# A Fourier and state-space encoder layer on one core: the norm weights folded into the input weights on the chip, and the split weights kept in device memory

## The chip, the core and the metric

The kernel runs on one core of a Trainium2 chip. The metric is the device time of one execution in microseconds, as the median of several runs. The engines are PE (TensorE, matrix products; PEld is its loading of the stationary operand), DVE (VectorE), ACT (ScalarE), POOL (GpSimd) and SP (SyncE, which here issues nearly all DMAs, in order). Each engine works through its own instructions in order; semaphores join them.

## What is computed

Two sequences (1024 and 2048 tokens, 1024 wide) go through one layer. Each is normalised, projected by one matrix `w_in`, and split into five parts:

```python
def rms_norm(x, w):
    y = xf * lax.rsqrt(jnp.mean(xf * xf, axis=-1, keepdims=True) + EPS)
    return (y * w).astype(x.dtype)

u = rms_norm(h, norm_w)
proj = u @ w_in
z_f, u_f, z_s, xbc, dt_raw = jnp.split(proj, [512, 1024, 2560, 5120], axis=-1)
```

`u_f` goes through a two-dimensional Fourier transform and a small mixing matrix, gated by `z_f`. `xbc` goes through a convolution of five taps and SiLU and becomes `x` (24 heads of 64), `B` and `C` (4 groups of 128); `dt_raw` (24 forward and 24 backward steps) becomes `dt` by a softplus. From these a state-space recurrence is computed forward and backward in chunks of 128 tokens, gated by `z_s` and normalised by group. Both results go through an output projection, a residual, a gated embedding and a last norm. All is in float32, to that precision.

## The kernel before

Products in float32 are made of three passes over numbers rounded for PE (float32r): a matrix `a` is split into `ah`, its rounding, and `al`, the rest, and a product is `ah bh + ah bl + al bh`. So an input weight of 1024 x 128 is split once into `wh` (a cast on ACT, L189) and `wl` (a subtraction on POOL, L190), and the normalised tokens into `uh` (ACT, L267) and `ul` (DVE, L268).

Stage 1 goes over three blocks of 1024 tokens: block 0 is the short sequence, blocks 1 and 2 the halves of the long one. Within a block the tokens lie turned (features on partitions) in three thirds of at most 342 columns, `uh0` to `uh2` and `ul0` to `ul2`, of which there is one copy each. The projection is cut into jobs of 128 output columns (`class Job`): four of `C`, four of `B`, twelve of `x`, twelve of `z`, four each of `uf` and `zf`, and one of `dt`, which is narrower and has its split weights in a tile of its own, `wdt`, loaded and split once for all blocks (L166 to L177). A job has three pieces, one for each third, of 24 matmuls (16 for `dt`) into one of three PSUM banks `ps`. That is 41 jobs or 123 pieces in a block.

The order of the work is written out by hand. One piece is a *slot*; `step` first issues what was put down for the slot with `pre`, then the piece, then what was put down with `post`. A *row* is a set of jobs whose pieces alternate, with a unit of the recurrence, the turn to the next block, or nothing attached to it. The first row of a block has `C`, `dt` and `B` (nine slots) and the chain of dt: `dt_turned` (transposes), `dt_softplus` in two parts (DVE), `dt_sums` (cumulative sums on PE, copied to `acs` by ACT, L471), `dt_rows` (transposes of `acs` on PE, `prw`, L493) and `dt_out` (stores to `ROWd` and `EXPd`). The last row of a block has `uf` 3 and `zf` 3 and brings in the next block's tokens: `x_in` loads a tile of 114 tokens, `x_norm` scales it (by the row's rstd and by the norm weight, `nwb`, in one DVE instruction, L250), `x_turn` transposes it into `uh` and `ul`.

A unit (two heads, twelve in a block) spreads over some twenty slots: rows of the decay, broadcast to all partitions, come in as `R` (L540), are cut by POOL (L548), go through an exponential on ACT (L558) and are joined on DVE (L563); POOL weights the tokens (`xw`, L587) for the states' products on PE (`pst`, L607); more rows (`er`, L635) and two outputs (L667, L669) go through SP.

Weights are loaded and split as many times as they are used, that is in every block: `weights_in` loads the raw columns into one tile `wr` (L182), `weights_split` makes `wh` and `wl`, of which there are two each. The plan (L746 to L758) splits a job's weights in the slot after the end of the job two before it, and loads the next job's raw columns one slot after a split:

```python
for m in range(2, len(coming)):
    j, k = coming[m], coming[m - 1]
    j.split_at = max(coming[m - 2].last + 1, k.split_at + 2)
    pre(k.split_at + 1, j.load)
    pre(j.split_at, j.split)
```

Tiles of the pool `t4` (six places) hold raw convolution inputs, x tiles, Fourier inputs and output weights in turn.

Stages 2 and 3 (the Fourier part; the output projection by Strassen-like sums; the embedding and the norm) are not touched.

Of the kernel before, what the change touches and what calls it, by code (L numbers as in the profile page):

```python
# [18 lines left out]
P = 128  # L19
DM = 1024  # L20
# [36 lines left out]
def tile_hybrid_encoder(ctx: ExitStack, tc: tile.TileContext, a):  # L57
# [20 lines left out]
    WSd = [dram.tile([P, 7, 4, 512], F32, name=f"WSd{i}") for i in range(3)]  # L78
    PLd = dram.tile([P, 2, DM], F32, name="PLd")
# [22 lines left out]
    with ExitStack() as ph:  # L102
        up = ph.enter_context(tc.tile_pool(name="up", bufs=1))
        wp = ph.enter_context(tc.tile_pool(name="wp", bufs=2))
        t4 = ph.enter_context(tc.tile_pool(name="t4", bufs=6))
# [19 lines left out]
        nwb = cp.tile([P, DM], F32, name="nwb")  # L125
# [35 lines left out]

        wdt = cp.tile([P, KT, 2, 64], F32R, name="wdt")

        def dt_weights_in():  # L166
            wdr = sp.tile([P, KT, 64], F32, tag="R1", bufs=3, name="wdr")
            V.memset(wdr, 0.0)
            for d in range(2):
                nc.sync.dma_start(  # L170
                    wdr[:, :, 32 * d:32 * d + 24],
                    w_in[:, C_DT + 24 * d:C_DT + 24 * (d + 1)].rearrange("(k p) c -> p k c", p=P))
            return wdr

        def dt_weights(wdr):
            S.copy(wdt[:, :, 0, :], wdr)
            V.tensor_tensor(wdt[:, :, 1, :], wdr, wdt[:, :, 0, :].bitcast(F32), op=ALU.subtract)  # L177

        def weights_in(c0):

            raw = wp.tile([P, KT, P], F32, tag="wr", bufs=1, name="wr")
            nc.sync.dma_start(raw, w_in[:, c0:c0 + P].rearrange("(k p) c -> p k c", p=P))  # L182
            return raw

        def weights_split(raw):

            wh = wp.tile([P, KT, P], F32R, tag="wh", name="wh")
            wl = wp.tile([P, KT, P], F32R, tag="wl", name="wl")
            S.copy(wh, raw)  # L189
            G.tensor_tensor(wl, raw, wh.bitcast(F32), op=ALU.subtract)  # L190
            return wh, wl
# [45 lines left out]

        def x_normed(b, i, xn):
# [11 lines left out]
            V.scalar_tensor_tensor(xt[:n, :], xt[:n, :], rs, nwb[:n, :], op0=ALU.mult, op1=ALU.mult)  # L250
# [61 lines left out]
        class Job:  # L312

            def __init__(self, B, kind, i):
                self.B, self.kind, self.i = B, kind, i
                self.c0 = {"C": C_C, "B": C_B, "x": C_X, "z": C_ZS, "uf": C_UF, "zf": C_ZF, "dt": None}[kind]
                if self.c0 is not None:
                    self.c0 += i * P
                self.dst = None
# [22 lines left out]
            def piece(self, si):  # L342
# [6 lines left out]
                if k == "dt":  # L349
                    for kt in range(KT):  # L350
                        passes = [(128, uh), (64, ul)]
                        for m, ut in passes if kt < KT - 1 else passes[::-1]:
                            T.matmul(ps[:m, :n], lhsT=wdt[:, kt, :, :].rearrange("p a c -> p (a c)")[:, :m],
# [376 lines left out]
        for bi, B in enumerate(blocks):  # L730
# [3 lines left out]
            rows_.append((B, [J("dt"), J("C"), J("B")] if bi else [J("C"), J("dt"), J("B")], "first"))  # L734
# [10 lines left out]

        n_, coming = 0, []  # L746
        for _, js, _ in rows_:
            for k, j in enumerate(js):
                j.last = n_ + 2 * len(js) + k
                if j.c0 is not None:  # L750
                    coming.append(j)
            n_ += 3 * len(js)
        coming[0].split_at = coming[1].split_at = -1
        for m in range(2, len(coming)):
            j, k = coming[m], coming[m - 1]
            j.split_at = max(coming[m - 2].last + 1, k.split_at + 2)
            pre(k.split_at + 1, j.load)
            pre(j.split_at, j.split)  # L758
# [627 lines left out]
```

## Time and profile before

| | us |
|---|---|
| median of three runs | 3041.28 |
| lowest, highest | 3039.87, 3051.15 |
| the profiled execution | 3031.59 |
| its span, first to last instruction | 3029.8 |

| engine | busy us |
|---|---|
| PE | 2836.0 |
| PEld | 2566.2 |
| DVE | 2228.9 |
| POOL | 1475.5 |
| ACT | 1389.1 |

The mean granted clock of TensorE is 0.972 of full speed. The profile is of one execution, and lines such as L361 are those of the kernel printed above. The views used below are the page (busy times, costliest groups), the busy times in stretches that one names, the list of who waited for whom (us in total, times, longest), the timeline (start, duration, engine, line, operation, result<-sources; in brackets the idle time before it and what ended it) and the list of DMA issues.

### The profile page before, as it was taken

To read this page: it belongs to the slowest core of one execution; us is meant where nothing else is said; L and a number is where in the kernel's file an instruction comes from. 1 tells how busy PE (TensorE), PEld (TensorE's weight loads), DVE (VectorE), ACT (ScalarE), POOL (GpSimd) and SP (SyncE) were. 2 spreads that over 40 slices of the span, in tenths; PEclk is the share of its full clock that TensorE was granted. 3 is DMA by queue.
4 is the path that set the end of the run, shared out by engine and by line. 5 is a ranking of instruction groups with operands and counts; after the bars stand their busy time and mean duration, and the time that the engine had idled before them with its cause. 6 is when DMAs were issued, how large, how long until landed. Compare 5 with 4: busy or idle time off the path is not lost. (4 is left out here: it accounts for less than half of the span.)

```text
span 3029.8 us, 47051 instructions
## 1 busy us (share of the span) xinstructions
PE 2836.0 (94%) x17252; PEld 2566.2 (85%) x17252; DVE 2228.9 (74%) x3412; ACT 1389.1 (46%) x2980; POOL 1475.5 (49%) x1114
## 2 busy tenths in 40 slices
PE   6899999989999899989999999969999899989998
PEld 6899989988999889989999999957677677768887
DVE  3687767666687568666779787687989988875665
ACT  4444545434544454434544444434433533354554
POOL 1355645431567565642555655455777578610000
PEclk9999999999999999999999999979999999999999
DMA  3378878972588778862677787566554644352221
GB/s 96 76 129 162 158 157 173 139 142 79 125 171 167 152 181 165 154 167 64 127 154 146 159 144 158 117 210 250 173 184 132 236 149 150 133 198 91 94 85 69
DMA packets 454579, 440.56 MB, mean 145 GB/s; under 512 B 24384, under 2 KB 405444, under 8 KB 450508
## 3 DMA queue, kind: packets, MB, share of 16 engines
q1 hardware_dynamic: 454060, 436.50, 60.6%
q8 instruction: 137, 2.24, 0.3%
q14 instruction: 94, 0.77, 0.1%
q10 hardware_dynamic: 288, 1.05, 0.1%
HBM read 328.41 MB, written 110.10 MB: 145 GB/s over the span
## 5 line engine op out<-in xcount | busy, mean ns | idle before, releaser
L361 PE MATMUL ps<-uh,wh 128*128 128x342 f32 (+1 forms) x2880 | 961.6, 334 | 8.4 <-ACT uh L267 8.4
L361 PE MATMUL ps<-ul,wh 128*128 128x342 f32 (+1 forms) x2880 | 926.3, 322 | 2.5 <-DVE ul L268 2.5
L361 PE MATMUL ps<-uh,wl 128*128 128x342 f32 (+1 forms) x2880 | 927.4, 322 | 0.4 <-POOL wl L190 0.4
L190 POOL TENSOR_TENSOR wl<-wr,wh 128x1024 fp32r<-128x1024 f32 x120 | 305.5, 2546 | 707.9 <-ACT wh L189 650.5
L361 PEld LDWEIGHTS ps<-uh,wh 128*128 128x128 f32 x2880 | 552.2, 192 | 20.1 <-ACT uh L267 9.2
L361 PEld LDWEIGHTS ps<-ul,wh 128*128 128x128 f32 x2880 | 554.5, 193 | 4.2 <-DVE ul L268 3.5
L361 PEld LDWEIGHTS ps<-uh,wl 128*128 128x128 f32 x2880 | 550.4, 191 | 1.2 <-POOL wl L190 1.1
L558 ACT ACTIVATE R<-R,lb 128x128 f32<-128x128 f32 x1152 | 356.8, 391 | 98.3 <-POOL R L548 98.2
L548 POOL TENSOR_SCALAR_AFFINE_SELECT R<-R 128x512 f32<-128x512 f32 x288 | 257.5, 905 | 193.7 <-DMA R<-ROWd 187.2
L618 DVE SCALAR_TENSOR_TENSOR H<-H,cd,pst 128x64 f32<-128x64 f32 x888 | 182.6, 274 | 47.7 <-PE pst L607 44.6
L402 DVE SCALAR_TENSOR_TENSOR xT<-raw,cvt,xT 128x1024 f32<-128x1024 f32 x144 | 214.8, 1492 | 2.6
L1102 PE MATMUL X<-whP,ah 128*128 128x512 f32 x480 | 195.2, 407 | 8.0 <-ACT pu L1111 6.4
L1102 PE MATMUL X<-wlP,ah 128*128 128x512 f32 x480 | 193.6, 403 | 1.6 <-DVE wlP L861 1.6
L1102 PE MATMUL X<-whP,al 128*128 128x512 f32 x480 | 192.5, 401 | 2.4 <-DVE al L1073 2.4
L587 POOL TENSOR_TENSOR xw<-xm,wd 128x512 f32<-128x512 f32 x144 | 181.8, 1268 | 18.7 <-PE pst L607 18.5
L367 ACT COPY raw<-ps 128x342 f32<-128x342 f32 x180 | 78.3, 438 | 241.7 <-PE ps L361 226.8
L1214 POOL TENSOR_TENSOR ht<-ht,pu 128x512 f32<-128x512 f32 x96 | 151.9, 1590 | 63.1 <-ACT pu L1111 43.0
L607 PE MATMUL pst<-xw,Bm 128*128 128x128 f32 x1056 | 151.3, 285 | 24.0 <-POOL xw L587 23.8
L607 PEld LDWEIGHTS pst<-xw,Bm 128*128 128x128 f32 x1056 | 131.9, 192 | 41.6 <-POOL xw L587 30.3
L189 ACT CAST wh<-wr 128x1024 fp32r<-128x1024 f32 x120 | 125.8, 1049 | 67.9 <-DMA wr<-in_w_in 67.2
L1073 DVE TENSOR_TENSOR al<-s,ah 128x512 fp32r<-128x512 f32 x144 | 143.6, 1021 | 16.4 <-ACT ah L1072 16.3
L563 DVE TENSOR_TENSOR R<-R,R 128x512 f32<-128x512 f32 x144 | 134.1, 931 | 25.9 <-ACT R L558 23.5
(264 smaller groups left out, 5703.9 us busy)
## 6 DMA issues: line engine op xcount, KB each, us to landing
R<-ROWd SPq DMA_DIRECT2D x288, 256.0 KB
wr<-in_w_in SPq DMA_DIRECT2D x120, 512.0 KB
er<-EXPd SPq DMA_DIRECT2D x288, 128.0 KB
Hd<-ht SPq DMA_DIRECT2D x48, 512.0 KB
ht<-Hd SPq DMA_DIRECT2D x48, 512.0 KB
y<-Yd SPq DMA_DIRECT2D x46, 512.0 KB
wlP<-WSd SPq DMA_DIRECT2D x21, 1024.0 KB
Yd<-y SPq DMA_DIRECT2D x72, 256.0 KB
```

Source lines behind the costliest of these rows:

```text
L190: G.tensor_tensor(wl, raw, wh.bitcast(F32), op=ALU.subtract)
L361: T.matmul(ps[:, :n], lhsT=wt[:, kt, :], rhs=ut[:, kt, :n], start=(i == 0), stop=(i == 3 * KT - 1))
L402: V.scalar_tensor_tensor(dst, raw[:, k:k + TB], cvt[:, 20 * k + ct:20 * k + ct + 1], dst, op0=ALU.mult, op1=ALU.add)
L548: G.affine_select(out=R.rearrange("p c h l -> p (c h) l"), in_=R.rearrange("p c h l -> p (c h) l"), pattern=[[0, 4], [sgn, P]], compare_op ...
L558: S.activation(R[:, c, h, :], R[:, c, h, :], AF.Exp, bias=self.B.lb[:, 2 * p + c, hc + h:hc + h + 1])
L563: V.tensor_tensor(E[0], E[0], E[1], op=ALU.add)
L587: G.tensor_tensor(xw, self.xm[c4].rearrange("p c (h e) -> p c h e", h=2), col(self.B.wd[:, c4:c4 + 4, hc:hc + 2]).broadcast_to([P, 4, 2, 6 ...
L607: T.matmul(pst[:, c, :], lhsT=B.Bm[self.g][:, c4 + c, :], rhs=xw[:, c, :, :].rearrange("p h e -> p (h e)"), start=True, stop=True)
L618: V.scalar_tensor_tensor(dst[:, e], H[d][:, cc, e], B.cd[:, cc, hc + h:hc + h + 1], pst[:, c, e], op0=ALU.mult, op1=ALU.add)
L1073: V.tensor_tensor(al, src, ah.bitcast(F32), op=ALU.subtract)
L1102: T.matmul(ps, lhsT=at[:, k, :], rhs=wt[:, k, :], start=(first and i == 0), stop=(i == 11), skip_group_check=not first)
L1214: return lambda t: G.tensor_tensor(h, h, t, op=ALU.add)
```

## The change

The norm weight is no longer multiplied into the tokens but into the rows of the input weights: it is loaded as eight rows of 128, turned on PE into `nwt`, a column for each of the eight k-tiles, and in block 0 each raw weight tile is scaled by eight ACT multiplies before its split. The tokens are scaled by their rstd alone, on ACT. In block 0 the split weights are stored to device memory (`WPd`, two slots after the split); in blocks 1 and 2 they are loaded from there, 2 x 512 KB in lines of 4 KB per partition, and cast in place on ACT, without POOL. There are three places for `wh` and for `wl`; in block 0 the raw tile takes one of the places of `wh`, so `wr` is gone, as are `nwb` and `wdt`; `t4` gets a seventh place. The weights of `dt` are a job's like the others. `B` has a row of its own behind the first row; in the last row the pieces are in another order; the slots of the dt chain, of the convolution of `C` 0 and of the x tiles are set anew.

```diff
+    WPd = {i: [dram.tile([P, KT, P], F32, name=f"WPd{i}_{x}") for x in range(2)] for i in range(C_DT // P)}
+    WPd["dt"] = [dram.tile([P, KT, P], F32, name="WPddt")]
...
-        wp = ph.enter_context(tc.tile_pool(name="wp", bufs=2))
-        t4 = ph.enter_context(tc.tile_pool(name="t4", bufs=6))
+        wp = ph.enter_context(tc.tile_pool(name="wp", bufs=3))
+        t4 = ph.enter_context(tc.tile_pool(name="t4", bufs=7))
...
-            V.scalar_tensor_tensor(xt[:n, :], xt[:n, :], rs, nwb[:n, :], op0=ALU.mult, op1=ALU.mult)
+            S.mul(xt[:n, :], xt[:n, :], rs)
...
+            def places(self):
+                return [wp.tile([P, KT, P], F32R, tag=f"w{x}", name=f"w{x}") for x in ("h" if self.dt else "hl")]
+
             def load(self):
-                self.raw = weights_in(self.c0)
+                if self.B.bi:
+                    self.w = self.places()
+                    for wt, kept in zip(self.w, self.kept):
+                        nc.sync.dma_start(flat(wt).bitcast(F32), flat(kept))
+                elif self.dt:
...
+                else:
+                    self.raw = wp.tile([P, KT, P], F32, tag="wh", name="wr")
+                    nc.sync.dma_start(self.raw, w_in[:, self.c0:self.c0 + P].rearrange("(k p) c -> p k c", p=P))
 
             def split(self):
-                self.w = weights_split(self.raw)
+                if self.B.bi:
+                    for wt in self.w:
+                        S.copy(flat(wt), flat(wt).bitcast(F32))
+                    return
+                raw = self.raw
+                for k in range(KT):
+                    S.mul(raw[:, k], raw[:, k], nwt[:, k:k + 1])
+                self.w = self.places()
...
+                S.copy(wh, raw)
+                (V if self.dt else G).tensor_tensor(wl, raw, wh.bitcast(F32), op=ALU.subtract)
+                for wt, kept in zip(self.w, self.kept):
+                    pre(slot[0] + 2, nc.sync.dma_start, flat(kept), flat(wt).bitcast(F32))
...
-                    conv(16 + i, self.dst, CT, s_ + (2 if i else 4))
+                    conv(16 + i, self.dst, CT, s_ + (2 if i else 3))
...
-            rows_.append((B, [J("dt"), J("C"), J("B")] if bi else [J("C"), J("dt"), J("B")], "first"))
+            rows_.append((B, [J("dt"), J("C")] if bi else [J("C"), J("dt")], "first"))
+            rows_.append((B, [J("B")], None))
...
+            if what == "last":
+                turn = [(0, 0), (0, 1), (1, 0), (0, 2), (1, 1), (1, 2)]
+            else:
+                turn = [(k, si) for si in range(3) for k in range(len(js))]
...
+            j = coming[m]
+            if j.B.bi:
+                pre(coming[m - 3].last + 1, j.load)
+                pre(max(j.first - 2, coming[m - 3].last + 2), j.split)
+            else:
+                j.split_at = max(coming[m - 2].last + 1, coming[m - 1].split_at + 2)
+                if m > 2:
+                    pre(coming[m - 1].split_at + 1, j.load)
+                pre(j.split_at, j.split)
...
-                    post(q + 7, dt_turned, B)
-                    pre(q + 8, dt_softplus, B, 0)
-                    pre(q + 9, dt_softplus, B, 1)
-                    post(s0 + 13, dt_sums, B)
-                    post(s0 + 14, dt_rows, B)
-                    pre(s0 + 16, dt_out, B)
+                    post(q + 5, dt_turned, B)
+                    pre(q + 6, dt_softplus, B, 0)
+                    pre(q + 7, dt_softplus, B, 1)
+                    post(q + 10, dt_sums, B)
+                    post(q + 12, dt_rows, B)
+                    pre(q + 14, dt_out, B)
...
-                    for i, s_ in enumerate((2, 3, 4, 4, 5, 6, 8, 9, 10)):
-                        pre(s0 + (0, 0, 1, 2, 2, 3, 5, 6, 7)[i], x_in, b, i)
+                    for i, s_ in enumerate((3, 4, 5, 5, 6, 7, 7, 8, 9)):
+                        pre(s0 + (0, 0, 1, 2, 3, 4, 5, 6, 7)[i], x_in, b, i)
```

More of the change, by code (lines that the diff above doesn't have):

```diff
@@ L123, in load_x @@
             return xt, n
-        nwb = cp.tile([P, DM], F32, name="nwb")
+        nwr = sp.tile([KT, P], F32, tag="y0", name="nwr")
+        nwt = cp.tile([P, KT], F32, name="nwt")
         tri = cp.tile([P, 2, P], F32, name="tri")
@@ L160, in tile_hybrid_encoder @@
         w_in = a["w_in"][0]
[L164 to L191, printed above, removed]
         def weight_sums(i, s0):
@@ L790, in tile_hybrid_encoder @@
             coming[0].split()
-            coming[1].load()
+            coming[2].load()
             x_in(b0, 5)
@@ L798, in tile_hybrid_encoder @@
             post(2, small_constants)
[L799 removed]
+            for i, (n_in, n_norm, n_turn) in enumerate(
+                    ((0, 0, 0), (0, 0, 0), (0, 0, 1), (0, 1, 2), (1, 2, 2), (1, 2, 3)), 3):
+                if i > 5:
+                    pre(n_in, x_in, b0, i)
                 if i > 3:
[L801 to L806 removed]
+                    pre(n_norm, x_norm, b0, i)
+                post(n_turn, x_turn, b0, i)
+            pre(8, decay_rates)
+            for (B, js, what), row in zip(rows_, pieces):
                 bi, s0 = B.bi, slot[0]
@@ L830, in tile_hybrid_encoder @@
                             pre(s0 + 2 * i, norm_piece, BLOCKS[bi + 1], i)
-                for si in range(3):
-                    for j in js:
-                        step(lambda: j.piece(si))
+                for j, si in row:
+                    step(lambda: j.piece(si))
             while before or behind_:
```

53 lines of the change are left out of this document (31 added, 22 removed).

## The prediction

> **What bounds the kernel now.** I read the page's busy times first, then the stretches of the program one by one, then PE's waits in each stretch, then the queues that feed them. The page names the engine:
>
> ```profile
> PE 2836.0 (94%) x17252; PEld 2566.2 (85%) x17252; DVE 2228.9 (74%) x3412; ACT 1389.1 (46%) x2980; POOL 1475.5 (49%) x1114
> ```
>
> PE is busy 94% of the span, and the change removes no matmul. So what it can win is PE's idle time, and the half-speed time that follows idling. The stretches (the first is the start up to the first `uf` job, then block 0, the turn to block 1, block 1, the turn to block 2, block 2, the two later stages, and a part of the last stage for a price) show where that is:
>
> ```profile
> 0.00:73.20 73.20, 48.07 (x273) 44.78 (x274) 25.67 (x51) 31.47 (x62) 7.84 (x9) 0.93 0.35 99
> 73.20:631.50 558.30, 538.09 (x3739) 518.16 (x3738) 404.97 (x681) 277.14 (x623) 281.56 (x220) 0.98 0.76 141
> 631.50:720.30 88.80, 79.22 (x537) 75.57 (x536) 51.84 (x90) 32.11 (x75) 26.78 (x20) 0.92 0.56 125
> 720.30:1300.50 580.20, 546.05 (x3761) 524.05 (x3759) 419.40 (x696) 276.52 (x619) 337.83 (x261) 0.98 0.74 153
> 1300.50:1389.10 88.60, 79.64 (x539) 75.78 (x539) 52.11 (x92) 32.25 (x75) 38.66 (x28) 0.92 0.51 137
> 1389.10:1937.60 548.50, 539.02 (x3781) 520.03 (x3780) 424.88 (x701) 256.33 (x584) 281.09 (x221) 0.99 0.69 139
> 1992.80:3029.80 1037.00, 969.84 (x4368) 773.79 (x4368) 818.64 (x1041) 468.08 (x904) 483.42 (x340) 0.97 0.45 153
> 2720.00:3020.00 300.00, 300.00 (x1397) 243.96 (x1396) 186.82 (x299) 156.08 (x302) 0.00 (x0) 1.00 0.24 83
> ```
>
> Columns: length; busy time of PE, PEld, DVE, ACT, POOL; granted clock; DMA share; GB/s. The same 108 slots (36 jobs of three pieces) take 558.3 us in block 0, 580.2 in block 1 and 548.5 in block 2, where PE idles 9.5 us. Block 1 idles 34 us, block 0 20 us. PE's waits in block 0, in the turn after it, in block 1 and in block 2 (total, times, longest):
>
> ```profile
> PE prw L493 <- ACT acs L471: 7.6, 1, 7.6
> PE pd L575 <- ACT wh L189: 3.9, 1, 3.9
> ...
> PE pst L607 <- POOL xw L587: 1.8, 3, 0.6
> ```
> ```profile
> PE pt L264 <- DVE H L618: 5.0, 2, 3.5
> PE pt L264 <- DVE xt L250: 4.4, 1, 4.4
> ```
> ```profile
> PE pst L607 <- POOL xw L587: 17.4, 11, 3.8
> PE pd L575 <- ACT wh L189: 6.2, 1, 6.2
> PE prw L493 <- ACT acs L471: 4.8, 1, 4.8
> ```
> ```profile
> PE prw L493 <- ACT acs L471: 4.8, 1, 4.8
> PE pst L607 <- POOL xw L587: 4.5, 4, 1.8
> ```
>
> Three things stand out: one wait for the cumulative sums of dt in each block (`acs`, L471), POOL's weighted tokens in block 1 (`xw`, L587), and a weight cast that ACT reached late (`wh`, L189). Each long wait costs more than itself, since the clock is halved around it; stretches at the first `acs` wait, at the second and at the `wh` wait of block 1:
>
> ```profile
> 103.30:110.10 6.80, 3.74 (x16) 3.48 (x17) 4.01 (x7) 4.88 (x8) 0.00 (x0) 0.50 0.00 0
> 748.40:755.20 6.80, 5.44 (x22) 5.17 (x23) 4.12 (x6) 6.01 (x10) 0.00 (x0) 0.50 0.00 1
> 1055.60:1062.40 6.80, 4.22 (x21) 3.92 (x22) 6.09 (x5) 2.00 (x5) 4.01 (x2) 0.50 0.82 130
> ```
>
> At clock 0.50, half of PE's busy time there is lost: 1.9, 2.7 and 2.1 us.
>
> **The dt chain.** Moving dt into a row with C alone, and B to its own row, keeps the number of slots but ends dt two slots sooner; the sums then come two slots ahead of the rows instead of one, and the softplus no longer runs against the taps of C and B at once on DVE. Two slots are about 10 us (580.2/108 = 5.4 us each), more than the longest wait, 7.6 us. In the three blocks this removes 7.6 + 4.8 + 4.8 = 17.2 us and 1.9 + 2.7 + 2.7 (the third taken as the second) = 7.3 us of clock: 24.5. I take -23, since ACT may still come late by a little; the other end is -12, if half of the waits only shrink. What is late next in these slots is DVE, whose softplus work is unchanged. The Trainium skill (TensorE: Matmul & The Clock Gate, Part 1) says that an idle window of about 3.4 us halves the clock and that a busy one of about 3.4 us restores it. By that alone each of the three waits would cost 1.7 us of clock, and this term would be 22.3 at most; the stretches above are 6.8 us wide, so the measurement decides.
>
> **The weights in blocks 1 and 2.** Each of the 40 split jobs of a block loses its subtraction on POOL and gains a second cast on ACT:
>
> ```profile
> L190 POOL TENSOR_TENSOR wl<-wr,wh 128x1024 fp32r<-128x1024 f32 x120 | 305.5, 2546 | 707.9 <-ACT wh L189 650.5 <-PE pst L607 36.6 <-PE po L649 9.2
> ```
> ```profile
> L558 ACT ACTIVATE R<-R,lb 128x128 f32<-128x128 f32 x1152 | 356.8, 391 | 98.3 <-POOL R L548 98.2
> L189 ACT CAST wh<-wr 128x1024 fp32r<-128x1024 f32 x120 | 125.8, 1049 | 67.9 <-DMA wr<-in_w_in 67.2
> ```
>
> POOL: 36 x 2.55 = 92 of 337.8 us go in block 1. More telling is the 650.5 us in which POOL, which works in order, stood before its subtraction until ACT had cast; `xw` and the row cuts are queued behind it. Without a subtraction nothing of POOL waits for a weight, and loads come four slots ahead instead of two, so the 67.2 us in which ACT stood before a cast for the DMA mostly go too. ACT gains 36 x 1.05 = 38 us on 276.5 of 580.2, which leaves it 46% idle. PE's 17.4 + 6.2 us in block 1 with 2.1 us of clock, 25.7 us, can go at most; I take -15, because R rows that land late delay POOL as well:
>
> ```profile
> POOL wl L190 <- ACT wh L189: 650.5, 102, 38.2
> POOL R L548 <- DMA R<-ROWd: 187.2, 106, 5.0
> ```
>
> Ends: -26 and +5 (the longer loads below delay R). Block 2 has 4.5 us of such waits: -2 (-4 to +6). The Trainium skill (SBUF — State Buffer, Who interferes with whom) says that a DVE instruction with two SBUF inputs and a POOL one that reads SBUF exclude each other for the whole instruction. By it the taps on DVE would win too, and block 1's term would go to its end, -26, and the sum to -35; no row here tells how much of DVE's time that is.
>
> **Block 0.** Here each job gains eight ACT multiplies of 128x128. The nearest row is L558, 356.8/1152 = 0.31 us each: 2.5 us per job, 89 us on ACT's 277 of 558. The cast, and POOL's subtraction behind it, end 2.5 us later, so `xw` behind those comes 2.5 us later; today that wait costs PE 1.8 us here, so a slack of a slot mostly covers it. SP's next raw load waits for the subtraction as it does now
>
> ```profile
> SPq L182 <- POOL wl L190: 409.3, 93, 34.1
> ```
>
> and the row, decay and output DMAs behind it on SP go 2.5 us later. Each job also stores 2 x 0.5 MB through SP, two slots after its split, when the subtraction on which the store waits is done; behind the store on SP are R's rows, on which POOL, then ACT's exponentials, DVE's join and PE's `pd` depend. The price of such a store is bounded by two rows: at the last stretch's 83/0.24 = 346 GB/s, 1.05 MB takes 3.0 us of all sixteen DMA engines; at block 0's 141/0.76 = 186 GB/s, 5.6 us. Over 36 jobs that is 109 or 203 us, against 24% of 558.3 = 134 us of unused DMA time. I take the lower price, since the stores are long contiguous lines as in the last stage: share 0.96. The queue then still keeps up, but R lands later. Estimate +12: a third of a microsecond per job, between 0 and +60. In blocks 1 and 2 a job loads 1.05 MB where it loaded
>
> ```profile
> wr<-in_w_in SPq DMA_DIRECT2D x120, 512.0 KB
> ```
>
> so 0.52 MB more, 1.6 us per job or 56 us per block of the 26% unused: covered.
>
> **The start.** The row's norm weight leaves DVE, and its scaling goes to ACT; the norm weight's broadcast load goes:
>
> ```profile
> 42.35 1.06 ACT L244 ACTIVATE junk<-xt 114x1024 bf16<-114x1024 f32 x1 [6.32 <-DMA xt<-in_x_prompt]
> ```
> ```profile
> 10.41 1.29 DVE L250 SCALAR_TENSOR_TENSOR xt<-xt,ss,nwb 114x1024 f32<-114x1024 f32 x1
> ```
> ```profile
> 21.29 0.65 PE L361 MATMUL ps<-uh,wh 128*128 128x342 f32 x1 [1.76 <-ACT uh L267]
> ...
> 29.72 0.40 PE L353 MATMUL ps<-uh,wdt 128*128 128x342 f32 x1
> ...
> 32.16 0.32 PE L353 MATMUL ps<-uh,wdt 128*128 128x342 f32 x1
> ...
> 44.65 0.65 PE L361 MATMUL ps<-uh,wh 128*128 128x342 f32 x1 [6.40 <-ACT uh L267]
> ```
>
> Ahead of the first piece ACT gets four multiplies (priced at L244's 1.06) and 2.5 us for C's weights, 6.7 us, less 2 us for the missing 0.5 MB load (1.5 to 2.8 us at the two rates above): +5. The 6.4 us wait at 44.65, due to an x tile that landed late, goes: the seventh t4 place and B's raw load, no longer held until C's split, bring x sooner; but ACT is then the bound and leaves 3 us of waits. Last, B is split only when C has ended: 2.5 + 1.05 + 2.55 = 6.1 us on ACT and POOL, covered by one dt piece of 2.8 us (29.72 to 32.48), so 3.3 us stick out. Sum +5 - 6.4 + 3 + 3.3 = +5; I take +4 (-5 to +12).
>
> **The turns.** The scaling of x moves to ACT there too, x gets later slots and PE has two pieces instead of three to cover each third. The waits on L250 and L618 go or change their name, new ones of 1 us or so arise ahead of each dt piece: 0, between -8 and +8 each. From 1992.8 on no line changes: 0.
>
> Sum: -23 - 15 - 2 + 12 + 4 = -24 us. The profiled execution took 3031.6 us, 9.7 under the median of 3041.28; -24 from the median is 3017.
>
> **Rivals.** *Block 0 becomes bound by DMA* (slower). Place: the stores among the R rows, in the queue that POOL already waits 187.2 us for. At 5.6 us per job the need is 203 - 134 = 69 us over what is free, in place of +12: the sum is +33, 3074. For it: R, broadcast rows, sets block 0's low rate. Against: the stores are not such rows. It decides from 4.7 us per job: 36 jobs then need 170 us, 36 more than are free, as much as the other terms bring. *ACT takes POOL's place* (no change): its work rises by 89 us in block 0 and 38 in each other block, PE's waits change their name to ACT, and block 1 keeps its 580: -24 + 15 + 2, -7, 3034. Against: ACT's idle half; for: `wh` waits exist. *The three places do not work as meant* (slower): if places go round in turn, a raw load of block 0 takes the place of the job two before, and SP stands until that job's last matmul, about two slots, with R queued behind it. Subtraction and `xw` then come a slot late; at 2 us per job for 36 jobs the sum is -24 + 72 = +48, 3089.
>
> **How the numbers follow.** A measurement can tell about 0.5% (15 us) from no change. Forecast 0.55, ACT 0.22, DMA 0.15, places 0.08. Of the forecast's 0.55 some 0.07 falls within 15 us; of ACT's 0.22, 0.06 is faster and 0.02 slower. So faster 0.54, same 0.22 (0.07 + 0.14 + 0.01), slower 0.24. The low end takes the gains whole (-24.5 - 26 - 4 - 5 = -59.5): 2982; the high end reaches into the DMA case: 3072. The forecast's own range, one term at a time at its far end, is 3001 (the turns) to 3037 (block 1).
>
> **What would show it.** Right: no wait on `acs`; block 1 within 570; POOL's busy time in block 1 near 246 us; POOL's wait for R in block 0 up by less than half; the first `uf` piece at 73 to 81 us. Wrong: DMA share of block 0 at 0.95 or more with PE idle over 40 us there; SP standing ten microseconds before each raw load; or waits on L189's successor on ACT as long as `xw` had.

## Result and profile after

The changed kernel took 3129.8 us (median of 4 runs, 3125.83 to 3149.84) against 3040.57 for the kernel before on the same chip: ratio 1.0301, 95% interval 1.0249 to 1.0352. It is 3% slower; the forecast was 3017, and its range ended at 3072. The profiled execution is the slowest of the four, 3149.84 us with a span of 3148.0, so its stretches add up to 118 us over before, not to the 89 between the medians.

First the engines' busy times on the page of the kernel after (its counterpart of before heads the prediction):

```profile
PE 2868.9 (91%) x17253; PEld 2599.0 (83%) x17253; DVE 2094.6 (67%) x3386; ACT 1590.6 (51%) x3417; POOL 1226.2 (39%) x1034
```

POOL lost 249 us of work, as it was meant to. DVE lost 134, of which the scaling of x (L250) is 37; nearly all the rest is the same instructions taking less time (last section). PE's share of the span fell from 94% to 91%. Then the stretches of the kernel after, with the columns of the prediction (start, block 0, turn, block 1, turn, block 2):

```profile
0.00:79.98 79.98, 49.79 (x275) 45.90 (x276) 16.29 (x48) 54.00 (x108) 7.80 (x9) 0.91 0.36 111
79.98:695.60 615.62, 555.26 (x3739) 532.04 (x3737) 401.59 (x677) 360.66 (x908) 278.58 (x220) 0.96 0.80 191
695.60:796.57 100.97, 79.64 (x537) 74.63 (x536) 46.62 (x90) 47.85 (x95) 17.91 (x17) 0.88 0.59 160
796.57:1384.03 587.46, 549.46 (x3761) 530.33 (x3759) 368.81 (x687) 307.57 (x652) 225.54 (x224) 0.97 0.75 181
1384.03:1485.62 101.59, 80.92 (x540) 75.56 (x539) 47.06 (x92) 47.28 (x90) 24.26 (x24) 0.88 0.60 156
1485.62:2045.57 559.95, 544.94 (x3783) 527.05 (x3781) 364.86 (x692) 290.22 (x621) 170.94 (x184) 0.98 0.70 169
```

Against before, the start is 7 us longer, block 0 57, the turns 12 and 13, block 1 7 and block 2 11. The remaining 10 us lie behind these stretches, nearly all in stages that no edit touches. That rest took 1089 to 1103 us in the sixteen profiles of this study, here 1102 against 1092, so its 10 us are scatter and not an effect of the change. Block 0 has the most: PE idles 60 us there (20 before), and its busy time is 17 us longer, since the granted clock stood at 0.50 for 51 us of the block (17 before). DMA is busy 80% of it. The waits of PE, POOL, ACT and SP in block 0 of the kernel after (total, times, longest):

```profile
PE pst L618 <- POOL xw L598: 41.9, 16, 5.5
```
```profile
POOL wl L334 <- ACT wh L333: 255.9, 34, 20.6
POOL R L559 <- DMA R<-ROWd: 57.0, 27, 6.0
```
```profile
ACT wr L327 <- DMA wr<-in_w_in: 69.8, 22, 7.9
```
```profile
SPq L318 <- POOL wl L334: 114.1, 29, 18.7
```

Read from below upwards, they close into a ring: SP waits for POOL's subtraction before it may load the next raw weights, ACT waits for the raw weights, POOL waits for ACT, and PE waits for `xw`, which is queued on POOL behind the subtraction. One round of it in the timeline of the kernel after (start, duration; in brackets the idle time before and what ended it), first POOL, then ACT, then SP:

```profile
309.27 2.40 POOL L334 TENSOR_TENSOR wl<-wr,wh 128x1024 fp32r<-128x1024 f32 x1 [3.54 <-ACT wh L333]
...
326.79 2.40 POOL L334 TENSOR_TENSOR wl<-wr,wh 128x1024 fp32r<-128x1024 f32 x1 [10.53 <-ACT wh L333]
```
```profile
323.18 2.45 ACT L327 ACTIVATE wr<-wr,nwt 128x128 f32<-128x128 f32 x8 [3.37 <-DMA wr<-in_w_in]
325.66 1.05 ACT L333 CAST wh<-wr 128x1024 fp32r<-128x1024 f32 x1
```
```profile
311.80 0.61 SPq L318 DMA_DIRECT2D wr<-in_w_in  x1
312.47 6.63 SPq L646 DMA_DIRECT2D er<-EXPd  x4
319.21 1.96 SPq L551 DMA_DIRECT2D R<-ROWd  x2
321.21 1.35 SPq L263 DMA_DIRECT2D WPd<-wh  x1
323.11 1.95 SPq L263 DMA_DIRECT2D WPd<-wl  x1
325.17 1.49 SPq L551 DMA_DIRECT2D R<-ROWd  x2
329.21 0.37 SPq L318 DMA_DIRECT2D wr<-in_w_in  x1
```

The subtraction ends at 311.67, the raw load goes out 0.13 us later, lands at 323.18 (11.4 us), multiplies and cast end at 326.71, the subtraction at 329.19, and the next load goes out at 329.21: 17.4 us for a round. Over the 35 raw loads of block 0 (issue and landing events of the trace) the mean round is 9.6 us of landing, 4.8 to the end of the cast, 2.5 to the end of the subtraction: 17.0, and 36 rounds are the 615.6 us of the block (17.1 each). In the kernel before the same means are 9.6, 3.2 and 2.6, 15.5 in all, and there the 3.2 hold spare time, since the cast takes 1.05. In the kernel after, multiplies and cast take 3.5 of the 4.8; in the rest the weights have landed and ACT has not come to them yet.

Block 1 looks different. There is no subtraction in it, and yet it got longer. Its waits on PE and on POOL:

```profile
PE pst L618 <- POOL xw L598: 11.8, 6, 2.8
PE pd L586 <- DVE R L575: 9.6, 2, 5.2
```
```profile
POOL R L559 <- DMA R<-ROWd: 309.5, 57, 44.9
```

`xw` fell from 17.4 us to 11.8, and the waits for `wh` and `acs` are gone, but PE now waits 9.6 us for what comes from R. POOL's 309.5 us are mostly spare time and no measure of that: POOL stood 51.2 us for R in the same block before and 174.5 for the cast, which is gone, and in the run e15 below it still stands 239.5 us for R where PE idles 10.

### The profile page after: what moved, and what is told of

The parts are those of the page before. It is cut to its first block, busy times and chain, and to the rows that moved or that the text cites. A ratio compares the mean times of both kernels' runs of the same rounds, so it can differ in the third digit from the quotient of the medians.

```text
span 3148.0 us, 47800 instructions
## 1 busy us (share of the span) xinstructions
PE 2868.9 (91%) x17253; PEld 2599.0 (83%) x17253; DVE 2094.6 (67%) x3386; ACT 1590.6 (51%) x3417; POOL 1226.2 (39%) x1034
## 3 DMA queue, kind: packets, MB, share of 16 engines
q10 hardware_dynamic: 288, 1.05, 0.1%
## 5 line engine op out<-in xcount | busy, mean ns | idle before, releaser
L559 POOL TENSOR_SCALAR_AFFINE_SELECT R<-R 128x512 f32<-128x512 f32 x288 | 232.1, 812 | 857.5 <-DMA R<-ROWd 732.2
L334 POOL TENSOR_TENSOR wl<-wr,wh 128x1024 fp32r<-128x1024 f32 x40 | 98.5, 2464 | 351.8 <-ACT wh L333 337.1
L618 PE MATMUL pst<-xw,Bm 128*128 128x128 f32 x1056 | 160.9, 297 | 66.3 <-POOL xw L598 66.0
L618 PEld LDWEIGHTS pst<-xw,Bm 128*128 128x128 f32 x1056 | 141.1, 204 | 83.8 <-POOL xw L598 74.9
L598 POOL TENSOR_TENSOR xw<-xm,wd 128x512 f32<-128x512 f32 x144 | 175.2, 1222 | 46.0 <-PE pst L618 36.6
L413 DVE SCALAR_TENSOR_TENSOR xT<-raw,cvt,xT 128x1024 f32<-128x1024 f32 x144 | 189.8, 1318 | 2.6
L663 DVE TENSOR_TENSOR yt<-po,er 128x512 f32<-128x512 f32 (+1 forms) x144 | 91.2, 634 | 87.8 <-PE po L660 66.0
```

What stands on the lines that cost most here:

```text
L334: (V if self.dt else G).tensor_tensor(wl, raw, wh.bitcast(F32), op=ALU.subtract)
L413: V.scalar_tensor_tensor(dst, raw[:, k:k + TB], cvt[:, 20 * k + ct:20 * k + ct + 1], dst, op0=ALU.mult, op1=ALU.add)
L559: G.affine_select(out=R.rearrange("p c h l -> p (c h) l"), in_=R.rearrange("p c h l -> p (c h) l"), pattern=[[0, 4], [sgn, P]], compare_op ...
L598: G.tensor_tensor(xw, self.xm[c4].rearrange("p c (h e) -> p c h e", h=2), col(self.B.wd[:, c4:c4 + 4, hc:hc + 2]).broadcast_to([P, 4, 2, 6 ...
L618: T.matmul(pst[:, c, :], lhsT=B.Bm[self.g][:, c4 + c, :], rhs=xw[:, c, :, :].rearrange("p h e -> p (h e)"), start=True, stop=True)
```

## Experiments

All edits are on the kernel after unless said otherwise. Where a stretch has the same instructions, its length repeats within 8 us: block 0 took 608.6 to 616.7 us in the six profiles that leave it untouched, block 1 584.0 to 588.7 in seven, block 2 554.3 to 560.0 in seven. Ratios are to the kernel before, timed beside each run. The fences of this section show stretches of the named kernel, columns as above. Some expectations count from other pieces: their turn of 126 us ends two jobs later than the 101 us of the fences, and their blocks 1 and 2 (562 and 559 us) begin there.

**Without the multiplies (e1).** The two lines `for k in range(KT): S.mul(raw[:, k], ...)` are out.

> The changed kernel without the eight multiplies per job that fold the norm weight in (so the norm weight is left out of the result); stores, places and all else stay. Read in block 0, from the first piece of uf to the turn, which took 558 us before and 616 us after. Theory A (ACT reaches the casts late, POOL stands before its subtraction and the weighted tokens stand behind it): block 0 comes back by 30 us or more, POOL's 256 us before wl fall under 150, PE's 42 us before xw under 15; total about 3090. Theory B (the stores fill the queue and make the raw weights and R late): block 0 comes back by less than 15 us, total 3115 or more. Theory C (the places: a raw load waits for the subtraction one job earlier, whatever ACT does): also less than 15 us.

3115.64 us, ratio 1.0265 (1.0234 to 1.0297).

```profile
72.75:671.02 598.27, 549.20 (x3738) 527.49 (x3737) 406.57 (x677) 273.78 (x616) 273.39 (x220) 0.97 0.83 194
```

Block 0 came back by 17 us, between what the theories asked, and the start by 7. POOL still stood 202.6 us before `wl`, PE 30.0 before `xw`, and ACT's wait for the raw weights rose from 69.8 to 101.1: with ACT quicker, the landing takes 10.9 us on the mean (9.3 in e3 below, which is without the stores too). The round is then 10.9 + 1.7 + 2.6 = 15.2 us, where a job takes 16.6: a raw load leaves SP 1.4 us after its place is free, so here the ring alone does not hold the block.

**Without the copies in device memory (e2).** No stores but dt's; blocks 1 and 2 load, scale and split like block 0.

> The changed kernel without the device-memory copies: no stores for any job but dt, and blocks 1 and 2 load, scale and split the raw weights as block 0 does. Theory A: block 0 stays near 600 us (under 15 back), and blocks 1 and 2 get slow like it, PE waiting 30 us or more in each for xw; total 3160 or more. Theory B: block 0 comes back to 575 or less, and blocks 1 and 2 are near 580 and 550; total 3080 to 3100. Theory C: block 0 hardly changes, blocks 1 and 2 get its lateness.

3113.89 us, ratio 1.0248 (1.0225 to 1.0271).

```profile
81.02:650.78 569.76, 540.74 (x3739) 518.06 (x3737) 398.35 (x677) 360.89 (x906) 286.67 (x220) 0.99 0.69 139
...
745.93:1350.42 604.49, 557.25 (x3761) 536.37 (x3759) 421.43 (x691) 361.76 (x908) 343.90 (x260) 0.95 0.73 146
...
1445.66:2014.38 568.72, 545.26 (x3782) 524.47 (x3781) 418.25 (x696) 343.40 (x875) 281.01 (x220) 0.98 0.71 134
```

The stores are worth 46 us of block 0 (615.6 to 569.8), more than theory A had left for them. The mean round is 7.9 + 5.3 + 2.6 = 15.8 us here, as long as a job: without the stores a raw weight lands in 7.9 us, with them in 9.6. The total falls by 16 us only, since blocks 1 and 2 now bear the multiplies.

**Neither (e3).** Both edits together.

> Neither the multiplies (norm weight left out) nor the device-memory copies: raw weights loaded, cast and split in every block as before the change, in the changed places and with the changed order of dt, the turns and x's scaling on ACT. If A and B together are the whole loss of block 0, block 0 is back at 550 to 565 us and what is left over against before are the turns (25 us) less the dt chain (20 us): 3035 to 3055. If the places are at fault (C), block 0 stays over 575 and blocks 1 and 2 go over 590 and 560: 3080 or more.

3042.09 us, ratio 1.0010 (0.9993 to 1.0027): no difference from before.

```profile
73.06:626.51 553.45, 536.58 (x3738) 517.48 (x3737) 406.77 (x677) 272.40 (x617) 282.00 (x220) 0.99 0.75 143
...
725.39:1299.14 573.75, 546.40 (x3761) 525.49 (x3759) 415.63 (x690) 274.11 (x617) 336.51 (x260) 0.98 0.74 153
...
1394.38:1938.18 543.80, 538.36 (x3782) 519.26 (x3781) 418.95 (x695) 255.99 (x585) 277.29 (x221) 1.00 0.70 139
```

The four runs make a square for block 0: 553.5 with neither, 569.8 with the multiplies, 598.3 with the stores, 615.6 with both. Multiplies cost 16 to 17 us and stores 45 to 46, each alike with and without the other (15 and 43 if the kernel after is taken at 613.0, the mean of the six profiles above); the places by themselves cost nothing (theory C, as far as it blames them alone, falls). In blocks 1 and 2 the multiplies would cost 31 and 25 us (e2 less e3), and what stands in their place, two loads and two casts for one load, a cast and a subtraction, costs 14 and 16 (after less e3).

**Raw weights by turns (e5).** This opens the ring in block 0: a raw load waits for the subtraction two jobs back.

```
-self.raw = wp.tile([P, KT, P], F32, tag="wh", name="wr")
+self.raw = wp.tile([P, KT, P], F32, tag="w" + "hl"[self.m % 2], name="wr")
...
-pre(coming[m - 1].split_at + 1, j.load)
+pre(max(coming[m - 1].split_at - 1, 0), j.load)
```

> The changed kernel with one edit for block 0: the raw weights take a third place of wh and a third place of wl by turns, and are loaded two slots earlier, so that a load waits for the subtraction two jobs back and not for that of the job before. Theory C (SP's 114 us before the raw loads and ACT's 70 us before the raw weights are the cause): both waits fall under 30 us, block 0 comes back by 25 us or more, total 3095 or less. Theory A (ACT's eight multiplies): the waits fall, but block 0 comes back by less than 15 us. Theory B (stores): the waits for the raw weights stay, moved to the queue.

3119.91 us, ratio 1.0261 (1.0228 to 1.0294). Block 0 and POOL's waits in it:

```profile
80.85:672.30 591.45, 549.04 (x3738) 527.32 (x3737) 393.00 (x677) 359.93 (x908) 270.73 (x220) 0.96 0.81 197
```
```profile
POOL wl L334 <- ACT wh L333: 168.4, 24, 24.5
POOL R L559 <- DMA R<-ROWd: 95.8, 39, 6.1
```

Block 0 came back by 24 us (21.5 from the mean of 613.0), just short of what theory C asked, and the total by 10 only, 25 short. SP's wait before the raw loads fell from 114 to 22 us, and ACT's for them is gone. The rest turned into a wait for R, where 57 us became 95.8, and into 31 us that POOL stood before the subtraction for stores to land. So the ring is one way in which the stores cost time, and R and the wait for the stores themselves are others.

**Stores on ACT's queue (e7), and the same with the ring open (e9).** `nc.sync.dma_start` becomes `nc.scalar.dma_start` for the stores, one slot later.

> The changed kernel with the stores of wh and wl issued from ACT, a slot later, and not from SP. The bytes and the sixteen DMA engines are the same; what differs is that the stores stand no more in SP's order and queue ahead of the R rows, the decays and the raw weights, at the price of ACT's time to issue them. Theory Q (the 45 us that the stores cost block 0 come from their place in SP's order and queue): block 0 comes back by 25 us or more, to 590 or less. Rival (the engines' bytes in a burst): by less than 10. Third (ACT's issue time and waits): block 0 gets longer, over 620.

> The run with raw weights by turns (block 0 there 591 us), with the stores issued from ACT a slot later. The ring of the raw weights is open in both, so what is left of the stores' cost must show in R. Theory (bytes): block 0 stays within 6 us of 591. Rival (SP's order: 1.1 us of SP's time for each store, ahead of R's loads): R's loads, 6.9 us after their slot there, come within 4.5 us and block 0 falls to 580 or less. Third (ACT's time to issue them): block 0 over 598.

e7: 3139.17 us, ratio 1.0320 (1.0297 to 1.0342), block 0 609.8: within the scatter, so theory Q falls while the ring is closed. A raw weight still lands in 9.5 us there, whichever engine issues the stores. e9: 3134.10 us, ratio 1.0308 (1.0278 to 1.0338); block 0, the wait of DVE that grew

```profile
81.89:701.16 619.27, 556.70 (x3738) 532.10 (x3737) 395.82 (x672) 359.61 (x911) 285.75 (x220) 0.95 0.76 189
```
```profile
DVE zT L248 <- ACT zT L247: 116.3, 12, 18.5
```

and, of ACT and of POOL,

```profile
ACT xT L417 <- DMA er<-EXPd: 70.9, 8, 12.9
```
```profile
POOL wl L334 <- DMA WPd<-wl: 116.0, 8, 18.4
```

R's loads did go out 2.4 us after their slot instead of 6.9, as the rival wanted, and the third theory held as well: ACT came late to its other work, DVE waited 116 us for `zT`, the gate's tile that ACT begins (35.5 in e5), and PE 52.5 us for the states `H` behind it on DVE. What ACT stood for is in the trace. The DMAs of this program, from SP and from ACT alike, use eight semaphores in turn, and an issue waits until the DMA that last used its semaphore has landed. ACT, done with its own work, stood 99 us before 19 of its stores, and each of these waits ended within 0.15 us of the landing of such an earlier load from SP (`er` for 90 of the 99 us). POOL, for its part, stood 116 us before the subtraction for stores of `wl` to land (31 us for stores in e5). The Trainium skill (DMA: Bandwidth & Descriptors, Queues, rings and completion order) says that each DMA engine takes turns between the queues that have work, packet by packet. No run here shows that by itself: R went out earlier because SP no longer issued the stores.

**No casts in blocks 1 and 2 (e8).** The matmuls read the kept weights as they land.

> The changed kernel without the two casts per job on ACT in blocks 1 and 2: the matmuls read the kept weights as they land (they were rounded when they were split). Block 0 is untouched. Blocks 1 and 2 (pieces 138 to 240 and 261 to 368) took 562 and 559 us, against 549 and 543 before. Theory (two casts, 2.1 us per job on ACT ahead of the exponentials): both come back by 8 us or more. Rival (the half megabyte more per job, and SP standing before the loads until a job's last matmul, make R late): both stay within 4 us.

3133.77 us, ratio 1.0297 (1.0274 to 1.0321). Block 1 580.5 and block 2 555.2, 7 and 5 us less, between what the theory and the rival asked, and in block 2 within the scatter: the casts are a small part at most.

**Kept loads from ACT (e10).** `nc.scalar.dma_start` for the loads of wh and wl in blocks 1 and 2.

> The changed kernel with the kept weights of blocks 1 and 2 loaded from ACT and not from SP; bytes, slots and casts as they are. In the changed kernel R's loads of block 1 were issued 8.2 us after their slot began on the mean, against 4.9 us in the kernel before with only the new dt order, and the block took 562 against 548 us. Theory (SP's order: the loads, standing until a job's last matmul, hold R's loads behind them): R's loads are issued within 6 us of their slot, blocks 1 and 2 come back by 6 us or more each, to 556 and 552. Rival (the bytes, whichever queue carries them): both within 3 us of 562 and 559. Third (ACT stands instead of SP and its exponentials come late): both longer by 5 us or more.

3163.04 us, ratio 1.0399 (1.0375 to 1.0423). Block 1, and PE's wait in it:

```profile
799.49:1404.98 605.49, 549.90 (x3760) 529.88 (x3759) 363.09 (x681) 302.22 (x653) 241.96 (x225) 0.95 0.74 177
```
```profile
PE po L660 <- DVE H L629: 54.6, 10, 11.7
```

R went out 2.6 us after its slot in block 1, from 8.2, and the block still got 18 us longer (block 2 six). The theory that SP's order alone is the cause falls; again ACT stood, 163 us before 32 of its loads, for earlier loads from SP to land, and `H` came late.

**One load per job (e15).** Blocks 1 and 2 load only wh.

```
-self.w = self.places()
-for wt, kept in zip(self.w, self.kept):
-    nc.sync.dma_start(flat(wt).bitcast(F32), flat(kept))
+self.w = [wp.tile([P, KT, P], F32R, tag="wh", name="wh")]
+nc.sync.dma_start(flat(self.w[0]).bitcast(F32), flat(self.kept[0]))
+if not self.dt:
+    self.w = self.w * 2
```

> The changed kernel, but in blocks 1 and 2 only wh is loaded for each job, 0.5 MB, and stands in for wl too (so wl's part is left out of those blocks); the cast runs twice on it, so that ACT's work is as before, and SP has one load per job to issue instead of two at the same slot. Theory (the bytes of the second load delay what is queued with them): blocks 1 and 2, 562 and 559 us in the changed kernel, come back by 12 us or more each, to 550 and 547 or less. Rival (the casts, and SP standing before a load until a job's last matmul): both within 5 us of 562 and 559.

3061.27 us, ratio 1.0052 (1.0035 to 1.0069).

```profile
789.71:1336.83 547.12, 536.66 (x3761) 518.21 (x3759) 368.18 (x687) 310.87 (x652) 228.89 (x224) 0.99 0.73 160
...
1430.45:1965.22 534.77, 534.77 (x3782) 517.67 (x3781) 364.87 (x692) 291.82 (x621) 167.22 (x184) 1.00 0.68 142
```

40 and 25 us less, with the casts as they were: the second half megabyte of each job is what blocks 1 and 2 pay for. In block 2 PE is busy without a gap. R's loads of block 1 went out 3.6 us after their slot. SP stood no less for a job's last matmul before these loads, 87 us in block 1 against 74 in the kernel after, so that part of the rival falls. The run takes out one DMA as well as its bytes, and these two are not told apart.

**The dt order alone (e4)**, on the kernel before: `[J("C"), J("dt")]` and `[J("B")]` as rows, the sums at q + 10 and the rows at q + 12, the x tiles of a turn at slots `(2, 3, 4, 4, 5, 6, 7, 8, 9)`.

> The kernel before with the new order of the dt chain alone: dt in a row with C, B in its own, the sums two slots ahead of the rows, and the x tiles turned at the slots that this order needs. Weights, scaling of x and the order of the last row are as before. Theory (the waits for the cumulative sums and the half clock after them are a real loss that the order takes away): no wait for acs in any block and 15 to 24 us less, 3015 to 3025. Rival (the dt pieces come sooner after the turn of x, and PE now waits there for uh instead): the acs waits go, waits on uh or xt of the same size come in the first six slots after the last row, total 3032 to 3042.

3027.48 us, ratio 0.9952 (0.9934 to 0.9970). From the start to block 2:

```profile
0.00:78.13 78.13, 48.40 (x275) 44.98 (x275) 30.45 (x57) 35.38 (x67) 7.82 (x9) 0.91 0.33 93
78.13:630.99 552.86, 536.38 (x3738) 516.96 (x3737) 405.17 (x676) 272.45 (x617) 280.93 (x220) 0.99 0.77 143
630.99:718.45 87.46, 78.19 (x537) 74.32 (x536) 58.93 (x96) 33.15 (x76) 26.60 (x20) 0.94 0.53 132
718.45:1291.67 573.22, 547.92 (x3761) 526.63 (x3759) 408.16 (x690) 274.46 (x617) 329.79 (x260) 0.98 0.76 154
...
1380.62:1919.71 539.09, 536.00 (x3783) 517.87 (x3781) 414.49 (x695) 254.92 (x583) 276.17 (x220) 1.00 0.68 141
```

The median is 14 us lower, just short of the theory's 15 to 24. The waits for `acs` are gone; blocks 0, 1 and 2 gain 5, 7 and 9 us, the turns do not lengthen, and the start, where x and dt now meet sooner, loses 5.

**x scaled on DVE (e6)** and **the turn's order (e11)**. e6 puts `V.tensor_scalar` in place of `S.mul` for x; e11 keeps ACT's scaling but runs the last row's pieces by turns as before and turns x at the slots of e4.

> The changed kernel with one edit: x is scaled on DVE again (by the row's norm alone) and not on ACT. It acts at the start and in the two turns only. Theory (ACT's scaling makes uh late there): the start, 80 us, falls under 77, each turn (from the last row's first piece to the end of dt and C, 126 us) falls by 4 us or more, total 8 to 15 us less. Rival (the new order and slots of the turn are the loss, whoever scales): both stay within 2 us, total unchanged.

> The changed kernel with the last row's pieces by turns as before the change, and the x tiles of the next block loaded, scaled (still on ACT) and turned at the slots of the kernel with the dt order alone, one slot sooner for the first five. Theory (the changed order frees the first third of x only after three pieces and turns it a slot later, so PE waits for uh ahead of dt and C): each turn, 126 us in the changed kernel, comes to 117 or less, total 15 to 25 us less than the changed kernel. Rival (ACT's scaling of x makes uh late at any slots): the turns stay over 122.

e6: 3129.66 us, ratio 1.0284 (1.0259 to 1.0310); the start is 76.3 us, the turns 100.3 and 95.1. e11: 3128.73, ratio 1.0278 (1.0246 to 1.0309), and its turns are

```profile
697.88:790.04 92.16, 79.48 (x537) 74.86 (x536) 47.48 (x90) 47.83 (x95) 18.44 (x17) 0.94 0.64 178
...
1378.73:1468.33 89.60, 79.53 (x539) 75.48 (x538) 47.27 (x93) 47.52 (x91) 24.14 (x24) 0.92 0.69 176
```

against 101.0 and 101.6: the order of pieces and slots gave 9 and 12 us back. Four other runs with the turns untouched by their edit (e1, e5, e7, e9) took 100.6 to 102.7 and 95.9 to 100.6, so of the second turn 6 to 12 us are the order's, and e6's 95.1 there is hardly outside the scatter. Scaling on DVE gave 4 us back at the start; an effect on the turns is not shown. The 21 us of e11's turns do not show in its median, which lies within the intervals of both; that its total is lower than the changed kernel's is not shown.

**Half of the store (e12).** The ring open in every block; kept is the scaled raw weight alone, 0.5 MB per job, and blocks 1 and 2 load it, cast it and subtract.

> As the run with raw weights by turns (block 0 there 591 us, blocks 1 and 2 560 and 554), but kept in device memory is only the scaled raw weight, 0.5 MB per job in place of 1 MB, stored as soon as it is scaled; blocks 1 and 2 load it, 0.5 MB in whole lines, and cast and split it as before the change, without multiplies. Theory (bytes: the megabyte stored per job delays raw weights and R): block 0 comes to 570 to 580, blocks 1 and 2, with the bytes of before, to 552 or less and 548 or less; total about 3060 to 3080. Rival (any store in SP's order costs the same, however long): block 0 stays over 585, blocks 1 and 2 come back all the same.

3013.32 us, ratio 0.9913 (0.9885 to 0.9941): faster than before, and 47 us lower than its theory allowed, which had left out what the open ring brings in blocks 1 and 2.

```profile
78.18:642.52 564.34, 541.60 (x3738) 519.81 (x3737) 393.64 (x677) 360.62 (x908) 281.28 (x220) 0.98 0.78 173
...
735.11:1287.80 552.69, 539.83 (x3760) 518.67 (x3759) 415.28 (x690) 273.08 (x617) 344.68 (x260) 0.99 0.78 158
...
1382.92:1918.27 535.35, 535.34 (x3782) 517.91 (x3781) 405.80 (x695) 254.69 (x585) 272.02 (x220) 1.00 0.69 141
```

Block 0 lost 27 of e5's 591 us with half of the store, and POOL's subtraction in blocks 1 and 2 does no harm: they are 35 and 25 us shorter than in the changed kernel, which was made to be rid of it.

**A version that beats both (e14).** The dt order with its turn, dt in a place, the ring open in every block, the norm weight on x, nothing kept but dt's weights.

> A version that could beat both: the new dt order with its turn, dt's weights in a place like the others, and the raw weights by turns in the third places, loaded two slots earlier in all blocks; the norm weight stays on x, on DVE, and no weights are kept but dt's. Theory (the ring raw load, landing, cast, subtraction, next raw load took 15.5 us per job before, as long as PE's three pieces; opened, it no longer holds PE): at least 8 us under the run with the dt order alone, 3008 to 3019. Rival (the ring only follows PE there, nothing is won, or R's rows are delayed by the earlier loads): 3022 to 3035.

2995.94 us, ratio 0.9854 (0.9831 to 0.9878), 31.5 us under e4's median and 12 under what its theory allowed.

```profile
73.98:621.02 547.04, 535.81 (x3738) 516.03 (x3737) 408.18 (x677) 272.03 (x617) 284.26 (x220) 0.99 0.75 144
...
711.62:1268.28 556.66, 541.16 (x3761) 520.44 (x3759) 417.30 (x690) 272.93 (x617) 339.13 (x260) 0.99 0.77 157
```

Against e4, from which it differs by the ring, the third places that open it, and dt's place, block 1 lost 17 us and block 0 six; PE's wait for `xw` in block 1 fell from 16.2 to 4.2 us. So the ring had held PE in the kernel before too, above all in block 1, as far as one run that changes the three together can tell.

## Why the prediction was wrong

**The bound** was read rightly: PE's work stayed (its instructions are the same), and all that was lost is PE idling and the slower clock around it.

**The dt chain**, -23: right in mechanism, too large. Alone it is worth 14 us (e4), and its start costs 5, which the prediction had not seen.

**Block 0**, +12: the step that failed most. "The queue then still keeps up, but R lands later. Estimate +12: a third of a microsecond per job" let the unused share of DMA time cover the stores. The price of the bytes was not at fault: DMA share times length rose by 2.3 us per job from e3 to e1 and by 2.8 from e2 to the kernel after, where the prediction took 3.0, and 17 to 20% of the DMA time stayed unused. Measured are 45 us for the stores, 1.25 us per job, and 16 for the multiplies, which "a slack of a slot mostly covers". There was no such slack: the prediction quoted SP's 409 us before the raw load and POOL's 650 before `wl` as two waits, and did not see that they follow on each other. Landing 9.6, cast 1.05 and subtraction 2.6 make 13.3 us of a 15.5 us round; 2.2 were free, the multiplies alone take 2.45, and the longer landing that the stores bring (7.9 to 9.6 us) comes on top.

**Blocks 1 and 2**, -15 and -2: of the wrong sign. "So 0.52 MB more, 1.6 us per job or 56 us per block of the 26% unused: covered" is the step that failed. The same half megabyte costs 40 and 25 us (e15), with 26% of DMA time unused before. That POOL's subtraction delays `xw` was true, but it was the ring that made it late: with the ring open, block 1 keeps the subtraction and takes 556.7 us (e14, in which dt has its place too).

**The start**, +4: +7, inside its bounds; the start is 73 us without the multiplies (e1, e3). **The turns**, 0 with at most 8 each: +12 and +13. "PE has two pieces instead of three to cover each third" was seen and priced at a microsecond; the order of pieces and slots is worth 9 us in the first and 6 to 12 in the second (e11).

**The rivals.** *Block 0 bound by DMA* was nearest in its sign and place, but not as told: it needed a DMA share of 0.95, and the share is 0.80. *ACT takes POOL's place* shows in the ring, not in blocks 1 and 2 (casts: 7 and 5 us). *The places do not work as meant*: in block 0 SP does not stand two slots for a job's last matmul (10.5 us in all for PE); the raw load leaves 0.13 us after the subtraction. The places did tie each load to the subtraction of the job before, as the single raw tile had done. The range missed because each cost was bounded alone, by busy shares, and none by the length of a round. It was also too narrow by the prediction's own terms: its end of 3072 lies below the prices of two rivals (3074 and 3089), and the forecast's own range to 3037 left out block 0's far end, which makes it 3065.

**The signs.** Three of the signs for being right came true although the forecast was 113 us off: no wait on `acs`, POOL's wait for R in block 0 up by less than half (48.1 to 57.0 us), the first `uf` piece at 80 us. Of the signs for being wrong, DMA's share stayed at 0.80, and SP stood 3.9 us before a raw load on the mean. None of these watched the round. Of the rest, block 1 at 587 us instead of within 570 told that the forecast was wrong.

**What stays open.** Whether it is the bytes or the number of DMAs that costs the 1.25 us per job, in the landing of the raw weights as in the lateness of R.

## What to carry to other kernels

When a buffer is loaded, worked on and freed in each job, add up one round, landing included, and set it against the time of a job: what is spare in the round is the slack, not the idle share of an engine or of the DMA. Extra traffic had a price per job here at a DMA share of 75 to 80%; half a megabyte cost 0.6 to 1.1 us of a job of 15 (45 us for two, 40 and 25 for one, over 36 jobs). A second buffer that breaks the round, which needs no more memory when two pools each have a spare place, was worth more here than taking away the work on it. Issuing DMAs from another engine also moved the standing before each issue into that engine's order (e9, e10).

## What the hardware showed unexpectedly

The stores lengthened the landing of the raw weights, 7.9 to 9.6 us (e2, after) and 9.3 to 10.9 (e3, e1), but hardly that of R, which they delayed in its issue. From issue to landing R's loads took 10.0 us on the mean in block 0 before and 10.2 after, 9.7 and 9.6 in block 1. Measured from the start of the slot in which they stand (mean over the 48 pairs of a block, the second load of each), they were issued 3.1 us late in block 0 before and 6.5 after, 5.6 and 8.2 in block 1. SP's DMA instructions did not grow long: the 364 of block 0 took 364 us, and 293 took 275 before, 1.00 us each against 0.94. There are more of them in the same order.

DVE's taps became faster where POOL's subtraction went. The group in block 1, first before, then after (busy time, mean ns, idle time before):

```profile
L402 DVE SCALAR_TENSOR_TENSOR xT<-raw,cvt,xT 128x1024 f32<-128x1024 f32 x48 | 75.3, 1568 | 0.9
```
```profile
L413 DVE SCALAR_TENSOR_TENSOR xT<-raw,cvt,xT 128x1024 f32<-128x1024 f32 x48 | 62.9, 1311 | 0.9
```

The rule of the Trainium skill (SBUF — State Buffer, Who interferes with whom) that the prediction weighed agrees with these rows, with 16% off each tap; in e12, which keeps the subtraction, a tap takes 1494 ns, and in e15, which has none, 1339. By that rule the sum would have been -35; DVE's gain was real, and not on the path.
